# Two adaLN modulation vectors in the first stage of an encoder trunk: from a split between TensorE and VectorE to TensorE alone

## The chip, the cores and the metric

One NeuronCore of a Trainium2 chip runs the whole program in one launch. The metric is the device time of that launch in microseconds (us).

## The reference, cut to what matters

A trunk of two layers works on x of 256 tokens by 2048 channels, in float32. Layer 0 is RWKV-7 time mixing and a squared-ReLU MLP, layer 1 is chunked band attention and an MLP. Every sub-layer normalizes x and modulates it by vectors that come from one conditioning vector c of 2048 numbers:

```python
mod = c @ w_ada[layer] + b_ada[layer]            # 2048 x 12288 weights per layer
sh1, sc1, gt1, sh2, sc2, gt2 = jnp.split(mod, 6, axis=-1)
...
h = modulate(rms_norm(x, g_mix[layer]), sh1, sc1)   # h * (1 + sc1) + sh1
y = rwkv7_time_mix(h, ...)                          # r, k, v = xr @ w_r, xk @ w_k, xv @ w_v, each 2048 x 2048
x = x + gt1[:, None, :] * y
```

The change is to how `sh1` and `sc1` of layer 0 are computed: two products of the vector c with 2048 x 2048 weights, 32 MB of weights in all. Nothing of layer 0 can be projected before the first channels of both are there.

## The kernel before, in words

Channels lie on the 128 partitions, so 2048 channels are 16 tiles (`KT`), and a tile of x is 128 x 256. The program is written with tile pools; a planner gives every instruction its place on its engine and sets the waits, so that the order on an engine is not always that of the text.

The change lies in `layer_a`, in the first stage of the kernel. The stage loads x into `h`, sums squares over channels on TensorE (L726, operand `ones`), makes the reciprocal root `r` of the mean square (`rstd`, L526 to L533), and then loops over the 16 tiles n. For each n:

- two loads are issued on the SP queue, `lw` (L781, the low-rank weights) and `raw` (L368 from L782, the rows of `w_v` that belong to tile n);
- `h` is scaled by `gain` and `r` on VectorE (L788) and shifted on ScalarE (L790);
- GpSimd makes the token difference `xx` (L734), VectorE the mixes `mix` (L739) and their high and low halves (L572, with ScalarE's L571);
- the weights are split into a rounded half `wH` on ScalarE (L378) and a rest `wL` on VectorE (L381);
- TensorE multiplies: `l` in plain float32 (L797, L801), and `v` in three products per 128 x 128 block (L805 to L807, 24 per tile).

From n = 4 on, each turn also does one `v_part` (two in the last two turns, two more after the loop): 24 products `t` (L767 to L769) for the other half of v's columns, summed in two PSUM tiles tagged `t` and `m`, which have one bank each, and added into `v` by VectorE (L777) or copied by ScalarE (L775). Its weights are a `raw` load of `w_v`. The tag `m` is also what `self.psm()` hands out.

`gain` and the shift `mods[(0, 0)]` come from a generator, `ada_blocks`, which takes channels in blocks of two tiles (seven blocks) and of one (two blocks), called from ahead of the loop and in each turn. It splits the sum over c's 2048 entries:

- the first 1024 entries go to TensorE: a tile of `crep` (c repeated over 32 columns) is the held operand and the weights move, 256 or 128 columns of them, in four 128 x 32 column tiles (L690). The 128 partial rows are copied out by ScalarE (`adat`, L701) and summed over partitions by matmuls of one moving column (L706);
- the other 1024 entries go to VectorE: a transposed copy of those weights (`w_ada0_t`) is multiplied by `crow` and summed along the row (L696, into `sums`). `crow` is c laid out along the free axis, made once at the start by `diag` (L665), two matmuls (L670) and two copies (L671).

VectorE adds both and the bias (L711, L713) and makes the gain (L715). The weights arrive in buffers `rawa` of 128 x 1024, six of them, loaded on SP (L686, L695): 64 loads of 512 KB.

The other modulation vectors are computed later in the kernel by VectorE into `acc` (L454) and summed over partitions by matmuls of one moving column in 128 x 32 tiles (L476), 32 matmuls at a time. Stage 2 begins with the projections at L412 and L413.

Of the kernel before, what the change touches and what calls it, by code (L numbers as in the profile page):

```python
# [12 lines left out]
F32 = mybir.dt.float32  # L13
F32R = mybir.dt.float32r
AF = mybir.ActivationFunctionType
ALU = mybir.AluOpType
AX = mybir.AxisListType

P = 128
D = 2048  # L20
T = 256
KT = D // P
# [8 lines left out]
HK = 8  # L31
# [298 lines left out]
class Body:  # L330
# [303 lines left out]
    def layer_a(self, st, sp):  # L634
# [6 lines left out]
        with ExitStack() as s1:  # L641
# [9 lines left out]
            for q in range(4):  # L651
# [2 lines left out]
            nc.scalar.dma_start(out=self.bada, in_=d["b_ada"])  # L654
            nc.scalar.dma_start(out=self.vecs, in_=d["vecs"])
            nc.scalar.dma_start(out=self.csts[:, first:], in_=d["cst"][:, first:])
            crep = pb.tile([P, HK, 32], F32, name="crep")
            nc.vector.tensor_copy(crep, self.ct[:, :HK].unsqueeze(2).to_broadcast([P, HK, 32]))
            nc.vector.memset(h[:, :, 0:1], 0.0)
            gain = self.gp.tile([P, KT], F32, name="gain_g_mix0")  # L660
            sums = pb.tile([P, 2, KT], F32, name="sums01")
            rawa = lambda: pb.tile([P, HK * P], F32, tag="rawa", bufs=6, name="rawa")

            crow, diag = self.wp.tile([P, HK * P], F32, tag="acc", bufs=1, name="crow"), rawa()
            nc.vector.tensor_tensor(out=diag.rearrange("p (k n) -> p k n", n=P),  # L665
                                    in0=self.cst("ident").unsqueeze(1).to_broadcast([P, HK, P]),
                                    in1=self.ct[:, HK:].unsqueeze(2).to_broadcast([P, HK, P]), op=ALU.mult)
            for i in range(0, HK * P, 512):
                ps = pp.tile([P, 512], F32, tag="t", bufs=1, name="t")
                nc.tensor.matmul(ps, self.cst("ones"), diag[:, i:i + 512], start=True, stop=True)  # L670
                nc.scalar.copy(crow[:, i:i + 512], ps)  # L671

            blocks = [2] * 7 + [1] * 2

            def ada_blocks():


                lo = 0
                for w_ in blocks:
                    W, ks = w_ * P, HK // w_  # L680
                    ps = self.psm().rearrange("p (i n) -> p i n", i=2)
                    for part in (1, 0):
                        w = d["w_ada0"][:, part * D + lo * P:part * D + lo * P + W].rearrange("(a i p) n -> a p i n", p=P, i=ks)
                        for a in range(w_):
                            raw = rawa().rearrange("p (i n) -> p i n", i=ks)
                            nc.sync.dma_start(out=raw, in_=w[a])  # L686
                            for i in range(ks):
                                kt = ks * a + i
                                g = 32 * (kt % 4)
                                nc.tensor.matmul(ps[g:g + 32, part, :W], crep[:, kt, :], raw[:, i, :],  # L690
                                                 start=(part == 1 and kt < 4), stop=(part == 0 and kt >= HK - 4),
                                                 tile_position=(0, g))
                            yield
                            raw = rawa()
                            nc.sync.dma_start(out=raw, in_=d["w_ada0_t"][KT * part + lo + a])  # L695
                            nc.vector.scalar_tensor_tensor(out=raw, in0=raw, scalar=1.0, in1=crow, op0=ALU.mult,  # L696
                                                           op1=ALU.mult, accum_out=sums[:, part, lo + a:lo + a + 1])
                            if part or a < w_ - 1:
                                yield
                    t = pb.tile([P, 2 * T], F32, tag="adat", bufs=1, name="adat").rearrange("p (i n) -> p i n", i=2)  # L700
                    nc.scalar.copy(t[:, :, :W], ps[:, :, :W])  # L701
                    ps = self.psm()
                    for part in range(2):
                        for i in range(w_):
                            for g in range(0, P, 32):
                                nc.tensor.matmul(ps[g:g + 32, 2 * part + i:2 * part + i + 1],  # L706
                                                 t[:, part, i * P + g:i * P + g + 32], self.col(C_32ND),
                                                 start=True, stop=True, tile_position=(0, g))
                    o = slice(lo, lo + w_)
                    part_sums = sums[:, :, o]  # L710
                    nc.vector.tensor_tensor(out=part_sums, in0=part_sums,  # L711
                                            in1=self.bada[:, :2 * KT].rearrange("p (b k) -> p b k", b=2)[:, :, o], op=ALU.add)
                    nc.vector.tensor_tensor(out=self.mods01[:, :, o], in0=part_sums,  # L713
                                            in1=ps[:, :4].rearrange("p (b i) -> p b i", b=2)[:, :, :w_], op=ALU.add)
                    nc.vector.scalar_tensor_tensor(out=gain[:, o], in0=self.mods[(0, 1)][:, o], scalar=1.0,  # L715
                                                   in1=self.vec("g_mix0")[:, o], op0=ALU.add, op1=ALU.mult)
                    lo += w_
                    yield

            ends = [sum(blocks[:i + 1]) for i in range(len(blocks)) for _ in range(blocks[i])]  # L720
            adab = ada_blocks()
            ss = pp.tile([P, 2, T], F32, tag="v3", bufs=1, name="v3")[:, 0, :]
            for n in range(KT):
                sq = pb.tile([P, T], F32, tag="sq", bufs=3, name="sq")
                nc.scalar.activation(sq, h[:, n, 1:T + 1], AF.Square)
                nc.tensor.matmul(ss, self.cst("ones"), sq, start=(n == 0), stop=(n == KT - 1))  # L726
            r = self.rstd(ss)
            adab_at = 4 * ends[0]
            for i in range(adab_at):
                next(adab)  # L730

            def diff(n):
                xx = ph.tile([P, T], F32, tag="xx", bufs=2, name="xx")
# [45 lines left out]
            for n in range(KT):  # L779
                lw = pb.tile([P, 448], F32, tag="lw1", bufs=3, name="lw1")  # L780
                nc.sync.dma_start(out=lw, in_=d["lora1"][n // 4, :, n % 4, :])  # L781
                raw = self.raw(d["w_v_rows"][n])  # L782
                ahead = 5 if n + 2 < KT and ends[n + 1] == n + 2 else 0
                while adab_at < min(4 * KT, 4 * ends[min(n + 1, KT - 1)] + ahead):
                    next(adab)
                    adab_at += 1
                hn = h[:, n, 1:T + 1]
                nc.vector.scalar_tensor_tensor(out=hn, in0=hn, scalar=gain[:, n:n + 1], in1=r,  # L788
                                               op0=ALU.mult, op1=ALU.mult)
                nc.scalar.activation(hn, hn, AF.Identity, bias=self.mods[(0, 0)][:, n:n + 1])  # L790
                xx = diff(n)
                first, last = n == 0, n == KT - 1
                self.split(xv, n, mixed(3, n, xx))
                H, L = self.halves(raw)

                for i, m in enumerate((1, 4)):
                    nc.tensor.matmul(pl[0][:96, i, :], lw[:, i * 96:(i + 1) * 96], mixed(m, n, xx),  # L797
                                     start=first and i == 0, stop=last and i == 1)
                t = mixed(5, n, xx)
                for i in range(2):  # L800
                    nc.tensor.matmul(pl[1][:, i, :], lw[:, 192 + i * P:192 + (i + 1) * P], t,  # L801
                                     start=first and i == 0, stop=last and i == 1)
                for i in range(8):
                    ps = pv[i // 2][:, i % 2, :]
                    nc.tensor.matmul(ps, H[:, i, :], xv[:, n, 0, 0:T], start=first and i % 2 == 0, stop=False)  # L805
                    nc.tensor.matmul(ps, H[:, i, :], xv[:, n, 1, 0:T], start=False, stop=False)
                    nc.tensor.matmul(ps, L[:, i, :], xv[:, n, 0, 0:T], start=False, stop=last and i % 2 == 1)  # L807
                if n == 3:
                    self.v_next = v_part_weight()
                for _ in range((n >= 4) + (n >= KT - 2)):  # L810
                    v_part()
                self.split(xk, n, mixed(2, n, xx))

                nc.vector.scalar_tensor_tensor(out=hn, in0=xx, scalar=self.vec("mu0", n), in1=hn,
                                               op0=ALU.mult, op1=ALU.add)
# [347 lines left out]
def _arrange(x, c, w_ada, b_ada, g_mix, g_mlp, w_up, w_down,  # L1163
# [16 lines left out]
    for i, w in ((0, rwkv_w2), (1, rwkv_a2)):  # L1180
# [16 lines left out]
        "cst": CST,  # L1197
        "vecs": f(np.stack(vecs).reshape(len(VECS), KT, P).transpose(2, 0, 1)),
        "b_ada": f(np.concatenate([f(b_ada).reshape(-1), f(b_ada_kv).reshape(-1)]).reshape(-1, P).T),
        "w_ada0": f(w_ada[0][:HK * P, :2 * D]),  # L1200
        "w_ada0_t": f(w_ada[0][HK * P:, :2 * D].T).reshape(2 * KT, P, HK * P),
        "w_ada": f(w_ada), "w_ada_kv": f(w_ada_kv),
        "w_up": np.stack([_pack(w) for w in f(w_up)]),
        "w_down": np.stack([_pack(w) for w in f(w_down)]),
# [27 lines left out]
```

## Time and profile before

| | us |
|---|---|
| median of 3 runs | 2667.99 (2667.93 to 2668.28) |
| the profiled execution, time | 2668.82 |
| the profiled execution, span of the trace | 2667.0 |
| TensorE busy | 2594.2 |
| VectorE busy | 2112.8 |
| ScalarE busy | 1345.2 |
| GpSimd busy | 208.7 |

The span runs from the first to the last instruction of the trace. Engines are PE (TensorE matmuls), PEld (its weight loads), DVE (VectorE), ACT (ScalarE), POOL (GpSimd) and SP, whose queue issues most loads. A group of instructions is shown by line, engine, operation and operands, then its count, busy time, mean duration in ns, the idle time of the engine ahead of it and what ended that idle time. A matmul in plain float32 leaves two records. A matmul's record lasts longer than the distance to the next one, since they are pipelined, so costs on TensorE are read from the distances between starts.

### The profile page before, as it was taken

The numbers are of one execution on the slowest core, as the hardware profiler recorded it, in microseconds if no ns is written. First come the engines' busy times: TensorE is split into PE (matmuls) and PEld (weight loads), VectorE is DVE, ScalarE is ACT, GpSimd is POOL, SyncE is SP. The second block draws the span as 40 slices with busy tenths as digits, with TensorE's granted clock in tenths as the row PEclk, the third lists the DMA queues.
The fourth block names the chain that finished last, engine by engine and source line by source line (L and its number), as shares of the span: only waits on it lengthen the run. The fifth ranks groups of instructions, "written<-read, shape, count | busy, mean of one in ns | idle before, by whom it ended". The sixth has DMA issues, their size and how long they took to land.

```text
span 2667.0 us, 58173 instructions
## 1 busy us (share of the span) xinstructions
PE 2594.2 (97%) x23596; PEld 2229.2 (84%) x23596; DVE 2112.8 (79%) x3102; ACT 1345.2 (50%) x2435; POOL 208.7 (8%) x320
## 2 busy tenths in 40 slices
PE   7999999999999999999999999999999999999997
PEld 4787777887899888888888998877898888888886
DVE  6788888889789888888888898899887555555555
ACT  3346455555456445355365554565564463453554
POOL 0002223322110000000001100000100000000002
PEclk9999999999999999999999999999999999999998
DMA  9976556566778888889898679887766555555553
GB/s 349 312 244 211 185 179 207 180 214 199 246 236 312 309 317 327 319 324 332 318 329 293 238 242 331 318 274 256 265 218 235 190 189 184 188 189 186 186 189 119
DMA packets 207149, 662.62 MB, mean 248 GB/s; under 512 B 21408, under 2 KB 54560, under 8 KB 206880
## 3 DMA queue, kind: packets, MB, share of 16 engines
q1 hardware_dynamic: 204816, 656.36, 71.5%
q8 instruction: 185, 3.03, 0.5%
q10 hardware_dynamic: 2064, 2.54, 0.3%
q14 instruction: 84, 0.69, 0.1%
HBM read 656.72 MB, written 2.10 MB: 247 GB/s over the span
## 4 chain that ended last, share of the span: by engine, by line
PE 85%; DVE 5%; issue 4%; DMA 4%; ACT 2%; POOL 1%; DVEq 0%; SPq 0%; ACTq 0%; POOLq 0%
PE pj L412 45%; PE pj L413 23%; PE pj L402 2%; PE pj L401 2%; PE pj L403 2%; DMA raw<-w_ada 1%; DVE wL L381 1%; PE iv L111 1%; DVE acc L454 1%; PE gr L105 1%; ACT wH L378 1%; PE ms L115 1%; PE o L401 1%; PE ms L324 0%; PE ms L105 0%
## 5 line engine op out<-in xcount | busy, mean ns | idle before, releaser
L381 DVE TENSOR_TENSOR wL<-raw,wH 128x1024 fp32r<-128x1024 f32 x772 | 941.1, 1220 | 354.9 <-ACT wH L378 347.0
L378 ACT CAST wH<-raw 128x1024 fp32r<-128x1024 f32 x772 | 805.8, 1045 | 799.7 <-PE pj L412 650.0
L412 PE MATMUL pj<-aHL,wH 128*128 128x512 f32 x3328 | 1202.0, 403 | 1.9 <-DVE x L945 1.4
L413 PE MATMUL pj<-aHL,wL 128*128 128x256 f32 x3328 | 936.1, 281 | 0.4 <-DVE wL L381 0.4
L412 PEld LDWEIGHTS pj<-aHL,wH 128*128 128x128 f32 x3328 | 629.4, 189 | 154.4 <-issue 8.7
L412 PE MATMUL pj<-hHL,wH 128*128 128x512 f32 x2048 | 723.0, 398 | 0.0
L413 PEld LDWEIGHTS pj<-aHL,wL 128*128 128x128 f32 x3328 | 629.4, 189 | 3.1 <-issue 0.8
L413 PE MATMUL pj<-hHL,wL 128*128 128x256 f32 x2048 | 574.4, 281 | 0.0
L412 PEld LDWEIGHTS pj<-hHL,wH 128*128 128x128 f32 x2048 | 384.6, 188 | 94.4 <-DVE hHL L991 0.2
L413 PEld LDWEIGHTS pj<-hHL,wL 128*128 128x128 f32 x2048 | 386.8, 189 | 0.1
L454 DVE SCALAR_TENSOR_TENSOR acc<-rada,ct,acc 128x1024 f32<-128x1024 f32 x256 | 327.2, 1278 | 8.5 <-DMA rada<-w_ada 7.6
L518 POOL TENSOR_TENSOR ss<-ss,sq 128x256 f32<-128x256 f32 x56 | 52.6, 940 | 1590.8 <-ACT sq L517 1590.5
L1016 DVE SCALAR_TENSOR_TENSOR x<-pj,mod,x 128x256 f32<-128x256 f32 x256 | 123.4, 482 | 58.6 <-PE pj L413 54.9
L454 DVE SCALAR_TENSOR_TENSOR acc<-raw,ct,acc 128x1024 f32<-128x1024 f32 x104 | 136.2, 1309 | 15.3 <-DMA raw<-w_ada 14.9
L988 ACT ACTIVATE t<-t 128x256 f32<-128x256 f32 x112 | 46.8, 418 | 123.5 <-DVE t L960 123.5
L401 PE MATMUL pj<-aHL,wH 128*128 128x258 f32 x384 | 109.0, 284 | 0.0
L402 PE MATMUL pj<-aHL,wH 128*128 128x258 f32 x384 | 108.9, 284 | 0.0
L403 PE MATMUL pj<-aHL,wL 128*128 128x258 f32 x384 | 108.0, 281 | 0.0
L403 PEld LDWEIGHTS pj<-aHL,wL 128*128 128x128 f32 x384 | 73.2, 191 | 0.2
L402 PEld LDWEIGHTS pj<-aHL,wH 128*128 128x128 f32 x384 | 72.6, 189 | 0.1
L401 PEld LDWEIGHTS pj<-aHL,wH 128*128 128x128 f32 x384 | 72.2, 188 | 0.2
L990 ACT ACTIVATE t<-t 128x256 f32<-128x256 f32 x128 | 53.4, 417 | 3.4
(249 smaller groups left out, 2815.5 us busy)
## 6 DMA issues: line engine op xcount, KB each, us to landing
raw<-w_up SPq DMA_DIRECT2D x256, 512.0 KB, 4.2
raw<-w_down SPq DMA_DIRECT2D x256, 512.0 KB, 4.3
rada<-w_ada SPq DMA_DIRECT2D x209, 512.0 KB, 5.8
raw<-w_ada SPq DMA_DIRECT2D x111, 512.0 KB, 4.3
rada<-w_ada_kv SPq DMA_DIRECT2D x64, 512.0 KB, 6.1
rawa<-w_ada SPq DMA_DIRECT2D x32, 512.0 KB, 6.9
rawa<-w_ada_t SPq DMA_DIRECT2D x32, 512.0 KB, 7.5
raw<-w_k SPq DMA_DIRECT2D x32, 512.0 KB, 4.0
```

What stands on the lines that cost most here:

```text
L378: nc.scalar.copy(Hf, raw)
L381: eng.tensor_tensor(out=Lf, in0=raw, in1=Hf, op=ALU.subtract)
L401: nc.tensor.matmul(ps, H[:, i, :], a(kt)[:, 0, :], start=(first and kt == 0), stop=False)
L402: nc.tensor.matmul(ps, H[:, i, :], a(kt)[:, 1, :], start=False, stop=False)
L403: ins = nc.tensor.matmul(ps, L[:, i, :], a(kt)[:, 0, :], start=False, stop=(last and kt == KT - 1))
L412: nc.tensor.matmul(ps, H[:, i, :], a(kt), start=(kt == 0), stop=False)
L413: ins = nc.tensor.matmul(ps[:, 0, :], L[:, i, :], a(kt)[:, 0, :], start=False, stop=(kt == KT - 1))
L454: nc.vector.scalar_tensor_tensor(out=self.acc, in0=raw, scalar=ck, in1=self.acc, op0=ALU.mult, op1=ALU.add)
L518: (eng or nc.gpsimd).tensor_tensor(out=self.ss, in0=self.ss, in1=sq, op=ALU.add)
L988: nc.scalar.activation(t, t, AF.Relu)
L990: nc.scalar.activation(t, t, AF.Square)
L1016: nc.vector.scalar_tensor_tensor(out=x, in0=ps[:, i, :], scalar=self.mods[(layer, 5)][:, n:n + 1], in1=x, op0=ALU.mult, op1=ALU.add)
```

## The change

The generator, `crep`, `crow`, `diag`, `sums`, `adat` and the transposed copy of the weights go. A function `mods_tile(n)` computes both vectors for one channel tile on TensorE: the weights, packed so that a partition's row of a load is one run of 4 KB, are the held operand, cut into 128 x 32 tiles, and one column of c moves. All 16 blocks of c and both vectors' sums are accumulated in two columns of one PSUM tile. VectorE adds the bias and makes the gain. `rawa` has seven buffers. `mods_tile(0)` stands ahead of the loop, `mods_tile(n + 1)` in turn n.

```diff
-            crep = pb.tile([P, HK, 32], F32, name="crep")
-            nc.vector.tensor_copy(crep, self.ct[:, :HK].unsqueeze(2).to_broadcast([P, HK, 32]))
...
-            crow, diag = self.wp.tile([P, HK * P], F32, tag="acc", bufs=1, name="crow"), rawa()
-            nc.vector.tensor_tensor(out=diag.rearrange("p (k n) -> p k n", n=P), ...
-                nc.tensor.matmul(ps, self.cst("ones"), diag[:, i:i + 512], start=True, stop=True)
-                nc.scalar.copy(crow[:, i:i + 512], ps)
-            blocks = [2] * 7 + [1] * 2
-            def ada_blocks():
...
+            def mods_tile(n):
+                ps = self.psm()[:, :2]
+                for part in (1, 0):
+                    for a in range(KT // HK):
+                        raw = pb.tile([P, HK * P], F32, tag="rawa", bufs=7, name="rawa")
+                        nc.sync.dma_start(out=raw, in_=d["w_ada0"][KT * part + n][:, a * HK * P:(a + 1) * HK * P])
+                        for i in range(HK):
+                            kt = HK * a + i
                             for g in range(0, P, 32):
+                                nc.tensor.matmul(ps[g:g + 32, part:part + 1], raw[:, i * P + g:i * P + g + 32],
+                                                 self.ct[:, kt:kt + 1], start=(part == 1 and kt == 0),
+                                                 stop=(part == 0 and kt == KT - 1), tile_position=(0, g))
+                m = self.mods01[:, :, n]
+                nc.vector.tensor_tensor(out=m, in0=ps, in1=self.bada[:, :2 * KT].rearrange("p (b k) -> p b k", b=2)[:, :, n],
+                                        op=ALU.add)
+                o = slice(n, n + 1)
+                nc.vector.scalar_tensor_tensor(out=gain[:, o], in0=self.mods[(0, 1)][:, o], scalar=1.0,
+                                               in1=self.vec("g_mix0")[:, o], op0=ALU.add, op1=ALU.mult)
...
             r = self.rstd(ss)
-            adab_at = 4 * ends[0]
-            for i in range(adab_at):
-                next(adab)
+            mods_tile(0)
...
                 raw = self.raw(d["w_v_rows"][n])
-                ahead = 5 if n + 2 < KT and ends[n + 1] == n + 2 else 0
-                while adab_at < min(4 * KT, 4 * ends[min(n + 1, KT - 1)] + ahead):
-                    next(adab)
-                    adab_at += 1
+                if n < KT - 1:
+                    mods_tile(n + 1)
...
-        "w_ada0": f(w_ada[0][:HK * P, :2 * D]),
-        "w_ada0_t": f(w_ada[0][HK * P:, :2 * D].T).reshape(2 * KT, P, HK * P),
+        "w_ada0": _pack(w_ada[0][:, :2 * D]),
```

More of the change, by code (lines that the diff above doesn't have):

```diff
@@ L656, in layer_a @@
             nc.scalar.dma_start(out=self.csts[:, first:], in_=d["cst"][:, first:])
-            crep = pb.tile([P, HK, 32], F32, name="crep")
-            nc.vector.tensor_copy(crep, self.ct[:, :HK].unsqueeze(2).to_broadcast([P, HK, 32]))
             nc.vector.memset(h[:, :, 0:1], 0.0)
             gain = self.gp.tile([P, KT], F32, name="gain_g_mix0")
-            sums = pb.tile([P, 2, KT], F32, name="sums01")
-            rawa = lambda: pb.tile([P, HK * P], F32, tag="rawa", bufs=6, name="rawa")
@@ L664, in layer_a @@
-            crow, diag = self.wp.tile([P, HK * P], F32, tag="acc", bufs=1, name="crow"), rawa()
[L665 to L670, printed above, removed]
-                nc.scalar.copy(crow[:, i:i + 512], ps)
@@ L673, in layer_a @@
-            blocks = [2] * 7 + [1] * 2
-            def ada_blocks():
[L678 to L704, printed above, removed]
-                            for g in range(0, P, 32):
[L706 to L718, printed above, removed]
@@ L720, in layer_a @@
-            ends = [sum(blocks[:i + 1]) for i in range(len(blocks)) for _ in range(blocks[i])]
-            adab = ada_blocks()
+            def mods_tile(n):
[6 more added lines that the diff above has]
+                            kt = HK * a + i
+                            for g in range(0, P, 32):
+                                nc.tensor.matmul(ps[g:g + 32, part:part + 1], raw[:, i * P + g:i * P + g + 32],
[7 more added lines that the diff above has]
+                                               in1=self.vec("g_mix0")[:, o], op0=ALU.add, op1=ALU.mult)
```

## The prediction

> **What bounds the kernel now.** I read the page first, then the chain of waits that ended last, then the stretches of the stage that the change touches, then that stage's groups on TensorE (PE) and VectorE (DVE), and last the order in time around single bursts.
>
> ```profile
> PE 2594.2 (97%) x23596; PEld 2229.2 (84%) x23596; DVE 2112.8 (79%) x3102; ACT 1345.2 (50%) x2435; POOL 208.7 (8%) x320
> PE 85%; DVE 5%; issue 4%; DMA 4%; ACT 2%; POOL 1%; DVEq 0%; SPq 0%; ACTq 0%; POOLq 0%
> 0.00:32.61 32.61, 18.21 (x117) 10.01 (x117) 13.21 (x26) 12.46 (x26) 2.38 (x6) 0.94 0.91 314
> 32.61:66.37 33.76, 28.87 (x253) 22.34 (x249) 28.60 (x61) 11.05 (x19) 3.78 (x4) 0.90 1.05 382
> 66.37:173.03 106.66, 97.22 (x904) 78.28 (x904) 87.64 (x173) 35.46 (x58) 7.22 (x9) 0.98 0.90 309
> 66.37:203.10 136.73, 124.67 (x1112) 104.17 (x1112) 110.39 (x207) 53.36 (x82) 8.14 (x10) 0.99 0.81 276
> ```
>
> The first row is busy time by engine, the second the chain by engine: the kernel is a TensorE kernel. The others are stretches: length, busy us of PE, PEld, DVE, ACT and POOL, the granted clock of PE, the share of the DMA engines and GB/s. The cuts are where the first `l` matmul of tile 0 starts (32.61), that of tile 4 (66.37), that of tile 14 (173.03), and stage 2's first matmul (203.10). After 203.10 the program is the same, so what the stage gains or loses is taken as what the kernel does. From 66.37 to 173.03 three things run close together: PE 97.2 of 106.7 us, DVE 87.6, DMA 0.90. DMA is not the limit there, having moved 382 GB/s in the stretch before against 309.
>
> A busy PE hides waiting, so its need is counted from starts. Groups from 66.37 to 203.10 (busy, mean ns, idle before and who ended it):
>
> ```profile
> L767 PE MATMUL t<-aHL,wH 128*128 128x256 f32 x125 | 36.6, 293 | 5.6 <-DVE v L777 4.2 <-ACT v L775 1.3
> L769 PE MATMUL t<-aHL,wL 128*128 128x256 f32 x125 | 36.1, 290 | 4.2 <-DVE wL L381 4.2
> L806 PE MATMUL v<-aHL,wH 128*128 128x256 f32 x96 | 27.3, 294 | 0.0
> L797 PE MATMUL l<-mix,lw 128*96 128x256 f32 x48 | 13.6, 405 | 2.6 <-DVE mix L739 2.6
> L690 PE MATMUL m<-rawa,crep 128*32 128x256 f32 x128 | 10.7, 406 | 0.0
> L690 PE MATMUL m<-rawa,crep 128*32 128x128 f32 x64 | 2.6, 279 | 0.0
> L706 PE MATMUL m<-csts,adat 128*32 128x1 f32 x160 | 2.3, 173 | 0.3 <-ACT adat L701 0.3
> ```
>
> And the order in time on PE (start, length, count), around a burst of L690, around one of L706, and over one tile's `l`:
>
> ```profile
> 71.91 0.28 PE L806 MATMUL v<-aHL,wH 128*128 128x256 f32 x1
> 72.02 0.28 PE L807 MATMUL v<-aHL,wL 128*128 128x256 f32 x1
> 72.23 0.64 PE L690 MATMUL m<-rawa,crep 128*32 128x256 f32 x8
> 73.02 0.29 PE L807 MATMUL v<-aHL,wL 128*128 128x256 f32 x1
> ...
> 105.78 0.28 PE L805 MATMUL v<-aHL,wH 128*128 128x256 f32 x1
> 105.99 0.43 PE L706 MATMUL m<-csts,adat 128*32 128x1 f32 x32
> 106.58 0.28 PE L807 MATMUL v<-aHL,wL 128*128 128x256 f32 x1
> ...
> 98.42 1.02 PE L797 MATMUL l<-mix,lw 128*96 128x256 f32 x4
> 100.20 0.39 PE L767 MATMUL t<-aHL,wH 128*128 128x256 f32 x1
> ```
>
> Main matmuls start 0.12 apart. Between the last one ahead of the L690 burst (72.02) and the second after it (73.02) lie 1.00 us where two steps, 0.24, would do: a burst of eight costs 0.76, entering and leaving included. By the same reading a burst of L706 costs 0.80 - 0.24 = 0.56. A tile's `l` takes 100.20 - 98.42 = 1.78, say 1.9 with the slower step behind it.
>
> Need of PE from 66.37 to 203.10: 375 `t` (L768 is as many as its neighbours) and 288 `v` at 0.12, 79.6; 12 tiles' `l`, 22.8; 16 bursts of eight and 4 of sixteen at L690, 15.2 at 0.76; six bursts of L706, 3.4 at 0.56. Sum 121.0 of 136.7. So 15.7 is waiting, and 11.0 of it stands in the rows as waits for DVE (4.2, 4.2 and 2.6).
>
> **The change part by part.** *Removed from DVE:* the products at L696.
>
> ```profile
> L696 DVE SCALAR_TENSOR_TENSOR rawa<-rawa,crow 128x1024 f32<-128x1024 f32 x20 | 24.0, 1217 | 0.0
> ```
>
> That is 24.0 of DVE's 87.6 us up to tile 14, leaving 64 of 107, 60%. The small adds (two a tile in place of three a block) stay near nothing. ScalarE loses the copies `adat` and `crow`; it is under half busy, so that pays nothing by itself.
>
> *Removed from PE:* L690 and L706, 15.2 + 3.4 = 18.6 us for tiles 6 to 15 in this stretch.
>
> *Added to PE:* per tile 2 x 16 x 4 = 128 matmuls with one moving column, 256 records, in four loads of 64 records. The nearest work is L476, which has the same form and sends 64 records at once:
>
> ```profile
> 1176.52 0.28 PE L413 MATMUL pj<-aHL,wL 128*128 128x256 f32 x1
> 1176.87 0.28 PE L413 MATMUL pj<-aHL,wL 128*128 128x256 f32 x1
> 1177.08 0.71 PE L476 MATMUL m<-csts,acc 128*32 128x1 f32 x64
> 1178.06 0.28 PE L413 MATMUL pj<-aHL,wL 128*128 128x256 f32 x1
> ...
> 1177.58 0.20 PE L476 MATMUL m<-csts,acc 128*32 128x1 f32 x3
> 1177.62 0.17 PE L476 MATMUL m<-csts,acc 128*32 128x1 f32 x1
> ```
>
> From L413 to L413 across the burst is 1.19, without it 0.35: 0.84 a burst. Inside, (0.71 - 0.17) / 63 = 0.0086 a record. The last two rows are the same burst cut short at its front: its last three records lie (0.20 - 0.17) / 2 = 0.015 to (1177.62 - 1177.58) / 2 = 0.02 apart, twice the mean. I read that as a stock of instructions, waiting when the burst began, that has run out by then. So a tile costs 4 x 0.84 = 3.36 if its four bursts stand alone, 0.84 + 192 x 0.017 = 4.1 if they join and the slow step holds, and 0.84 + 192 x 0.0086 = 2.5 if they join and the fast one does. I take 3.36, since every L690 burst above stands alone between other matmuls, each behind its own load; 2.5 and 4.1 stay for the range. All sums of a tile go into two columns; L476's records, two to a sum, show no price for that.
>
> [...]
>
> *From 66.37 on, after:* 79.6 + 22.8 + 10 tiles x 3.36 = 136.0 with no wait at all, already the present 136.7. For waits I take 8 of the present 15.7: DVE's 11.0 halved as its load falls, the rest left; ends 3 and 13. Result 144.0, +7.3.
>
> *From 32.61 to 66.37:* the rows there, cold clock included (0.90 granted):
>
> ```profile
> L805 PE MATMUL v<-aHL,wH 128*128 128x256 f32 x32 | 9.9, 336 | 0.0
> L797 PE MATMUL l<-mix,lw 128*96 128x256 f32 x16 | 5.7, 491 | 2.7 <-DVE mix L739 2.7
> L690 PE MATMUL m<-rawa,crep 128*32 128x256 f32 x52 | 4.9, 447 | 0.0
> L769 PE MATMUL t<-aHL,wL 128*128 128x256 f32 x3 | 0.9, 316 | 1.6 <-DVE wL L381 1.6
> L706 PE MATMUL m<-csts,adat 128*32 128x1 f32 x64 | 0.9, 173 | 0.0
> ```
>
> Four tiles: 96 `v` and 9 `t` at 0.12, 12.6; `l` 7.6; 6.5 bursts of L690, 4.9; two of L706, 1.1: 26.2 of 33.8, 7.6 lost. After: 20.2 + 4 x 3.36 = 33.6, with 5 lost (ends 3 and 7.6) 38.6, +4.8.
>
> *Ahead of 32.61:*
>
> ```profile
> 13.35 1.91 PE L670 MATMUL t<-rawa,csts 128*128 128x512 f32 x2
> ```
>
> ```profile
> 26.36 1.22 DVE L696 SCALAR_TENSOR_TENSOR rawa<-rawa,crow 128x1024 f32<-128x1024 f32 x1
> 27.50 0.42 DVE L533 SCALAR_TENSOR_TENSOR rstd<-ru,rstd 128x256 f32<-128x256 f32 x1
> ```
>
> `crow`'s matmuls stand among the sums of squares (1.9), and the last step of `r` stands behind an L696 (1.1). Both go, and the first gain needs 2 MB of weights, not 4. I take 4 us earlier (0 to 6); what is late next is the loads, 7.9 MB by the second tile (x 2.1, constants and the first turn's loads 1.6, eight of `rawa` 4.2), 25 us at the 314 GB/s of that stretch.
>
> *Moved:* 64 loads of 512 KB stay 64 on SP, four in a row and ahead of the same turn's `w_v` load. They now wait for PE alone to free a buffer, seven in place of six; `lw` and both `raw` loads are queued behind that wait, and ScalarE's and VectorE's splits wait for these. `mods_tile` also takes the one bank `m` from `v_part` and must wait for L777; behind it on PE are `l`, `v` and the next `v_part`. Both are inside the waits above.
>
> *Sum.* With c the price of a tile: late 10c - 26.3, early 4c - 8.6, start -4, together 14c - 38.9. For c = 3.36 that is +8.1. The span goes from 2667.0 to 2675.1; the profiled execution took 2668.8 against a median of 2668.0, so the forecast goes on the median: 2676.1. Its own range, by waits 3 to 13 and 3 to 7.6 and a start 0 to 6 earlier: 2669 to 2688.
>
> **The rivals.** *Faster:* VectorE is the real pace-setter, the bursts join at 0.0086 (c = 2.5), and waits fall to 3 late and 4 early: 14c - 44.9 = -9.9, 2658. It decides below c = 3.2. For it: the 11.0 us of waits for DVE. Against: the slow last records, and L690's bursts that never join.
>
> *No change:* c = 3.36 with the same low waits, and a start 6 earlier: 14c - 46.9 = +0.1, 2668. For it: PE needs only 121 of 137 now. Against: `m`, the loads and the split of `raw` still make PE wait.
>
> *Fed too slowly:* bursts join, and the slow step rules: c = 4.1 gives +18.5, and at 0.02 a record c = 4.7 gives +27; 2691 in the middle. For it: the last three records. Against: it needs loads that are there ahead of time. [...]
>
> **How the numbers follow.** About 0.2%, 5 us, is what a measurement of this kernel can tell from no change. Chances: forecast 0.58 (0.50 slower, 0.08 within), faster 0.13 (0.12 faster, 0.01 within), no change 0.17 (0.14 within, 0.02 slower, 0.01 faster), fed too slowly 0.12. Together 0.13 faster, 0.23 the same, 0.64 slower. The range 2660 to 2697 leaves out some 0.07 below and 0.06 above.
>
> **What would show it.** Right: L696, L690 and L701 gone; 4096 records of one column on PE; a burst of 64 with 0.84 between its neighbours; DVE near 60% in the loop; waits for DVE under 6 us; stage 2's first matmul near 211 and the first `l` near 28.6. Wrong: joined bursts at under 0.01 a record, or that first matmul before 203 (faster); records 0.015 apart or more (slower still); or a difference that arises after stage 2 begins, which I take as none.

## The result, and the profile after

The changed kernel takes 2730.25 us (median of four, 2722.72 to 2733.2) against 2667.96 of the kernel before: ratio 1.023, interval 1.0208 to 1.0253. It is 62 us slower; 8 were forecast, and the time lies outside the range of 2660 to 2697. The profiled execution took 2733.2 us, with a span of 2731.4.

From the page of the changed kernel, busy time by engine and the row of TensorE's instruction queue (packets, MB):

```profile
PE 2636.2 (97%) x27144; PEld 2282.8 (84%) x27144; DVE 2073.2 (76%) x3041; ACT 1340.4 (49%) x2424; POOL 212.5 (8%) x320
...
q8 instruction: 213, 3.49, 0.5%
```

The same queue on the page of before:

```profile
q8 instruction: 185, 3.03, 0.5%
```

TensorE has 3548 matmul records and as many weight loads more, some 7100 instructions; its queue fetched 28 packets more, 0.46 MB, so a packet is 16 KB and holds about 256 instructions, and 185 of them fit the 47192 records of before.

Nearly all of the loss lies in the stage that was changed (62.0 of the 64.4 us between the two profiled spans). Stage 2's first matmul starts at 265.04 (before 203.09). The first `l` starts at 36.1 (before 32.6, +3.5), tile 4's at 82.5: the early stretch, from the first `l` to tile 4's, takes 46.4 (33.8, +12.6), the late one, from there to stage 2, 182.5 (136.7, +45.8). The stretches of the changed kernel, cut about there, and below them three around one place of it (length, busy us of PE, PEld, DVE, ACT and POOL, granted clock, DMA share, GB/s):

```profile
0.00:34.50 34.50, 15.97 (x543) 13.59 (x544) 3.68 (x9) 9.69 (x21) 0.83 (x5) 0.90 0.91 323
34.50:83.00 48.50, 38.76 (x919) 33.93 (x915) 22.11 (x52) 10.38 (x18) 3.87 (x4) 0.79 0.69 241
83.00:265.00 182.00, 157.71 (x3574) 142.03 (x3573) 89.61 (x170) 51.51 (x76) 10.13 (x11) 0.86 0.62 211
...
101.00:106.00 5.00, 1.49 (x63) 1.39 (x53) 0.50 (x3) 0.00 (x0) 0.00 (x0) 0.66 0.90 347
106.00:116.00 10.00, 9.32 (x172) 8.18 (x171) 5.93 (x11) 3.70 (x6) 0.92 (x1) 0.83 0.34 101
116.00:129.00 13.00, 12.98 (x426) 11.20 (x427) 6.34 (x13) 3.70 (x6) 0.92 (x1) 1.00 0.86 306
```

VectorE is busy 49% of the late stretch, the DMA share has fallen to 0.62, and the granted clock from 0.99 to 0.86. So neither of the old neighbours of the bound holds the stage now. The waits from 20 to 265 us (us in total, times, longest):

```profile
DVE mods L673 <- PE m L669: 89.1, 16, 8.6
...
PEld m L669 <- issue: 35.9, 28, 4.6
PE m L669 <- issue: 29.3, 10, 4.6
...
PE t L722 <- DVE v L732: 1.5, 1, 1.5
PE t L722 <- ACT v L730: 1.4, 2, 0.7
```

TensorE hardly waits for VectorE any more. It stands mostly in front of its own new matmuls and waits for nothing that the trace shows ("issue"). The order in time on PE shows one such place (start, length, count), and, later, bursts that run through:

```profile
100.45 0.28 PE L758 MATMUL v<-aHL,wH 128*128 128x256 f32 x1
100.57 0.28 PE L759 MATMUL v<-aHL,wH 128*128 128x256 f32 x1
100.78 0.47 PE L669 MATMUL m<-ct,rawa 128*32 128x1 f32 x34
104.77 0.60 PE L669 MATMUL m<-ct,rawa 128*32 128x1 f32 x30 [3.51 <-issue]
105.30 0.58 PE L760 MATMUL v<-aHL,wL 128*128 128x256 f32 x1
105.68 0.41 PE L758 MATMUL v<-aHL,wH 128*128 128x256 f32 x1
...
188.41 0.28 PE L758 MATMUL v<-aHL,wH 128*128 128x256 f32 x1
188.62 0.71 PE L669 MATMUL m<-ct,rawa 128*32 128x1 f32 x64
189.26 0.67 PE L750 MATMUL l<-mix,lw 128*96 128x256 f32 x2
```

The burst at 188.62 (a burst is a run of such matmuls) takes 0.85 from the `v` ahead of it to the `l` behind. The one at 100.78 stops after 34 of its 64 records, though they read one load that is there, and goes on 3.7 us later. Counting PE's instructions from the start of the trace (matmuls, weight loads and its few semaphore instructions), this stop comes after 4033 of them, which is 193 more than a multiple of 256. There are 13 stops of 1.8 to 4.7 us, from the last start ahead to the first behind, and all come 193 past a multiple of 256; they take 38.6 us in all. Ten are inside bursts, three between main matmuls shortly behind one. The kernel before has no stop of 1 us or more at that place in this stage. In the stop at 101 the instruction queue fetched one packet (row of its queue from 101 to 106):

```profile
q8 instruction: 1, 0.02, 1.2%
```

It landed 1.4 us ahead of the next record. In each of the 13 stops one packet of that queue landed, 1.2 to 1.6 us ahead of the next record. Behind the stop the main matmuls start 0.21 apart, not 0.12, until 109.3: the granted clock of the rows 101 to 116, 0.66 and 0.83, and 0.50 from 102.7 to 109.4. I call a run of 256 instructions a block, and a stop at place 193 one at a block's end.

### The profile page after: what moved, and what is told of

It is laid out like the page before. It is cut to its first block, busy times and chain, and to the rows that moved or that the text cites. A ratio compares the mean times of both kernels' runs of the same rounds, so it can differ in the third digit from the quotient of the medians.

```text
span 2731.4 us, 65181 instructions
## 1 busy us (share of the span) xinstructions
PE 2636.2 (97%) x27144; PEld 2282.8 (84%) x27144; DVE 2073.2 (76%) x3041; ACT 1340.4 (49%) x2424; POOL 212.5 (8%) x320
## 4 chain that ended last, share of the span: by engine, by line
PE 87%; DVE 5%; DMA 3%; issue 3%; ACT 1%; POOL 0%; DVEq 0%; SPq 0%; ACTq 0%
PE pj L412 44%; PE pj L413 22%; DMA raw<-w_ada 2%; PE pj L402 2%; PE pj L401 2%; PE pj L403 2%; PE m L669 2%; DVE acc L454 2%; PE iv L111 1%; DVE wL L381 1%; PE v L758 1%; PE v L759 1%; PE gr L105 1%; PE v L760 1%; PE t L722 1%
## 5 line engine op out<-in xcount | busy, mean ns | idle before, releaser
L412 PEld LDWEIGHTS pj<-aHL,wH 128*128 128x128 f32 x3328 | 629.5, 189 | 153.1 <-issue 8.2
L941 ACT ACTIVATE t<-t 128x256 f32<-128x256 f32 x112 | 46.8, 418 | 123.7 <-DVE t L913 123.7
L669 PEld LDWEIGHTS m<-ct,rawa 128*32 128x32 f32 x4096 | 44.0, 117 | 54.0 <-issue 45.2
L669 PE MATMUL m<-ct,rawa 128*32 128x1 f32 x4096 | 50.0, 175 | 39.7 <-issue 29.3
L402 PEld LDWEIGHTS pj<-aHL,wH 128*128 128x128 f32 x384 | 72.6, 189 | 0.1
```

Source lines behind the costliest of these rows:

```text
L402: nc.tensor.matmul(ps, H[:, i, :], a(kt)[:, 1, :], start=False, stop=False)
L412: nc.tensor.matmul(ps, H[:, i, :], a(kt), start=(kt == 0), stop=False)
L669: nc.tensor.matmul(ps[g:g + 32, part:part + 1], raw[:, i * P + g:i * P + g + 32], self.ct[:, kt:kt + 1], start=(part == 1 and kt == 0), st ...
L941: nc.scalar.activation(t, t, AF.Relu)
```

## The experiments

Edits are shown against the changed kernel, where no other is named.

**Half the price.** Every second block of c is left out.

```diff
-                        for i in range(HK):
+                        for i in range(0, HK, 2):
...
-                                                 stop=(part == 0 and kt == KT - 1), tile_position=(0, g))
+                                                 stop=(part == 0 and kt == KT - 2), tile_position=(0, g))
```

> The changed kernel with every second of c's 16 blocks left out of the two vectors; all 64 loads stay. Three theories of the 62 us. Supply: PE's instructions arrive in blocks of 256, about one per 5.8 us in this stage, and a turn of the loop needs 512 for the vectors and some 150 for the rest; halved, a turn needs 1.6 blocks, 9.3 us, less than PE's own 9.9, so the gaps at every 256th instruction nearly go: 2660 to 2675. Burst price (the prediction's c): bursts of 32 records at 0.56 in place of 0.84, 14 tiles x 1.12 = 16 us less than the changed kernel: 2714. Late loads: nothing changes, 2730.

Measured 2683.79 us, ratio 1.006 [1.0037, 1.0083]. One stop at a block's end is left (2.3 us at 22.9). The first `l` starts at 27.7, 4.9 earlier than before. So three quarters of the loss go with half the instructions, far more than a price by the record would give back; nearest is the theory of supply, but 16 us stay with hardly a stop, and no theory had that. Late waits of this run (63 to 224):

```profile
DVE mods L673 <- PE m L669: 49.5, 11, 5.6
...
PE t L722 <- DVE v L732: 8.6, 8, 1.4
PE l L750 <- DVE mix L694: 8.6, 10, 1.5
```

The order in time of one turn shows how they hang together:

```profile
123.19 0.43 PE L669 MATMUL m<-ct,rawa 128*32 128x1 f32 x32
...
123.70 0.16 DVE L673 TENSOR_TENSOR mods<-m,bada 128x2 f32<-128x2 f32 x1 [5.45 <-PE m L669]
...
124.09 0.48 DVE L741 SCALAR_TENSOR_TENSOR h<-h,gain_g_mix,rstd 128x256 f32<-128x256 f32 x1
...
127.27 1.27 DVE L694 SCALAR_TENSOR_TENSOR mix<-xx,vecs,h 128x256 f32<-128x256 f32 x3
```

VectorE stands 5.45 us for a tile's last burst, with `h`, the mixes and the adds into `v` queued behind; that tile's `l` follows 5 us after the burst. The last two experiments take this up.

**Held operands of 128 columns,** a quarter of the matmuls.

```diff
-                            for g in range(0, P, 32):
-                                nc.tensor.matmul(ps[g:g + 32, part:part + 1], raw[:, i * P + g:i * P + g + 32],
...
+                            nc.tensor.matmul(ps[:, part:part + 1], raw[:, i * P:(i + 1) * P],
...
```

> The changed kernel with one 128x128 held operand per block in place of four 128x32: same sums, a quarter of the matmuls (64 records a tile, not 256). Supply: no gap at every 256th instruction; what is left is the price of a tile, unknown for a 128-column load before one moving column, 0.06 to 0.12 a record, c of 4 to 8, and with 14c - 38.9 that is 2685 to 2741; PE's clock returns to 1.0. Burst price: the changed kernel plus 14 x (c - 3.36), 2739 to 2795. Late loads: 2730.

One run, 2846.93 us, slower than anything expected: all theories missed. No stop at a block's end is left, but a record is dear. Two stretches, and two bursts in order of time:

```profile
32.00:70.00 38.00, 36.24 (x182) 34.53 (x183) 13.13 (x31) 5.32 (x10) 1.87 (x3) 0.59 0.43 150
70.00:180.00 110.00, 98.56 (x567) 91.85 (x566) 31.17 (x66) 16.49 (x27) 3.06 (x5) 0.70 0.45 154
```

```profile
121.01 1.84 PE L668 MATMUL m<-ct,rawa 128*128 128x1 f32 x16
...
139.37 2.77 PE L668 MATMUL m<-ct,rawa 128*128 128x1 f32 x13
```

Inside the first the records start 0.112 us apart, inside the second 0.213 (the main matmuls ahead of it start 0.21 apart, those ahead of the first 0.12), against 0.0084 in 128 x 32 tiles; and PE, busy nearly all the time, is granted only 0.59 to 0.70. So this run says nothing on the supply of instructions. Why the clock falls there was not tried.

**No loads.** Tile 0's weights serve all tiles; the loads of the other fifteen are left out.

```diff
-                        raw = pb.tile([P, HK * P], F32, tag="rawa", bufs=7, name="rawa")
-                        nc.sync.dma_start(out=raw, in_=d["w_ada0"][KT * part + n][:, a * HK * P:(a + 1) * HK * P])
+                        if n == 0:
+                            kept[part, a] = pb.tile([P, HK * P], F32, name=f"rawa{part}{a}")
+                            nc.sync.dma_start(out=kept[part, a], ...)
+                        raw = kept[part, a]
```

> The changed kernel with the weights of tile 0 used for all 16 tiles, loaded once: 60 of 64 loads are left out, the instructions on PE stay. Supply, with the blocks' arrival slowed by the loads beside them: gaps stay at every 256th instruction but shrink, 2680 to 2705; supply that does not depend on the loads: 2725 to 2735. Burst price: 2725 to 2735 with no gaps inside bursts. Late loads: 2680 or less, no gaps.

One run, 2718.7 us: 30 MB less to load bring some 12 us. It lies between the two forms of the theory of supply (2680 to 2705, 2725 to 2735). Fifteen stops are left, all at the same place of a block, 1.2 to 3.6 us, 39.2 in all. Three of them follow on one another (PE in order of time):

```profile
28.83 1.89 PE L673 MATMUL m<-ct,rawa 128*32 128x1 f32 x128 [3.39 <-issue]
32.28 1.07 PE L673 MATMUL m<-ct,rawa 128*32 128x1 f32 x66 [1.57 <-issue]
...
35.74 1.45 PE L673 MATMUL m<-ct,rawa 128*32 128x1 f32 x94 [1.10 <-issue]
```

With the data at hand, 128 matmul records and 128 weight loads, a block, start every 3.45 us. So the stops need no late loads of these weights. That loads lengthen them is possible: the packets that end the stops start on average 1.5 us after the block before has begun to run here (counted from its place 193), and 3.4 us after that in the changed kernel.

**The disputed cost by itself.** The kernel before, with bursts of 16, 32, 64, 128 and 256 matmuls of the same form on constants, put between the projections of the MLPs, far from the changed stage.

```diff
+                if q == 2 and n in (2, 5, 8, 11, 14):
+                    pm, ones = self.psm(), self.cst("ones")
+                    for k in range(4 << (n // 3)):
+                        for i in range(0, P, 32):
+                            nc.tensor.matmul(pm[i:i + 32, 0:1], ones[:, i:i + 32], self.col(C_ONE), ...
```

> The kernel before with extra bursts of the change's form (128x32 held constants, one moving column, no load behind them) in the third quarter of both MLPs' down projections: 16, 32, 64, 128 and 256 matmuls, that is 32 to 512 records, with 128x128 work between them. Burst price at 0.017 a record beyond 64: 0.56, 0.84, 1.9, 4.1 and 8.5 us, 32 us in both layers, 2700; at 0.0086: 20 us, 2688. Supply of PE's instructions in blocks of 256, one per some 3.5 us when PE waits for them (the steps between the gaps where tile 0's weights were reused): no gap up to 64 records, then one for each block that runs out: the burst of 512 records, four blocks, takes 11 to 15 us, that of 256 some 4 to 8; 2700 to 2715, about alike in layer 0, where loads run at 320 GB/s, and layer 1, at 187.

One run, 2725.39 us. PE in order of time, around the bursts of 128 and 256 records in the first MLP and of 512 in the second:

```profile
1286.44 1.25 PE L1018 MATMUL m<-csts 128*32 128x1 f32 x128
1287.62 0.50 PE L412 MATMUL pj<-hHL,wH 128*128 128x512 f32 x1
...
1305.60 1.81 PE L1018 MATMUL m<-csts 128*32 128x1 f32 x197
1312.51 1.02 PE L1018 MATMUL m<-csts 128*32 128x1 f32 x59 [5.09 <-issue]
1313.46 0.79 PE L412 MATMUL pj<-hHL,wH 128*128 128x512 f32 x1
...
2507.80 1.48 PE L1018 MATMUL m<-csts 128*32 128x1 f32 x157
2512.62 1.88 PE L1018 MATMUL m<-csts 128*32 128x1 f32 x128 [3.34 <-issue]
2516.10 1.89 PE L1018 MATMUL m<-csts 128*32 128x1 f32 x128 [1.59 <-issue]
2519.58 1.55 PE L1018 MATMUL m<-csts 128*32 128x1 f32 x99 [1.59 <-issue]
```

128 records run through, from first to last start 1.07 us, 0.0084 each: only the last two steps are longer, 0.017, as they are in a burst of 64. The 256 stop after 197 (after 253 in the second MLP, 2.8 us), the 512 after 157. From then on exactly 128 records run and then 1.6 us pass: a block every 3.48 us (2512.62 to 2516.10 to 2519.58), the 1.9 of its own records included (1.25 in the burst at 1286.44). Each of these packets starts 1.1 us after the block before has begun to run and takes 1.0 us, and 1.4 us after it has landed the next record starts. So the price is a step: in these bursts nothing for the first 157 to 253 records, one to two blocks with their weight loads, and then a stop of 3 to 5 us and 1.6 to 1.9 at each block after that. This carries the theory of supply.

The time is 57 us above the kernel before, 10 above the highest that was expected. The eight stops take 24 of it and the 1984 records 17 at 0.0084. What is left, 16, was not taken apart; the clock rows of the trace show half clock for 48 us around these stops.

**TensorE alone, with few instructions:** the old form (L690's), `crep` held and the weights moving, for all sixteen blocks of c, six buffers.

```diff
-            def mods_tile(n):
...
+            blocks = [2] * 7 + [1] * 2
+            def ada_blocks():
...
+                        for a in range(2 * w_):
...
+                                nc.tensor.matmul(ps[g:g + 32, part, :W], crep[:, kt, :], raw[:, i, :],
+                                                 start=(part == 1 and kt < 4), stop=(part == 0 and kt >= KT - 4),
```

> VectorE left out as in the change, but by the form the kernel before has for its first half: all 16 blocks of c held, repeated over 32 columns, and the weights moving, 256 columns a matmul (six buffers). PE's price of a tile is the same as forecast for the change: eight bursts at 0.76 and one at 0.56 for two tiles, c = 3.3, but a quarter of the instructions. Supply: no gap at every 256th instruction; 14c - 38.9 is +8, and the longer waits for VectorE's mixes and sums that halving left (10 us more than before) may be in it: 2672 to 2690. If price or VectorE's absence alone made the 62 us: 2720 or more.

Measured 2686.87 us, ratio 1.0075 [1.0047, 1.0103]. No stop at a block's end; stage 2 begins at 221.8. The stretch from 66 on, and its idle times on PE:

```profile
66.00:222.00 156.00, 146.77 (x1400) 115.92 (x1399) 91.90 (x168) 57.21 (x88) 10.98 (x12) 0.98 0.80 259
```

```profile
L749 PE MATMUL t<-aHL,wH 128*128 128x256 f32 x128 | 38.1, 298 | 6.3 <-DVE v L759 4.1 <-ACT v L757 1.6 <-ACT wH L378 0.5
L751 PE MATMUL t<-aHL,wL 128*128 128x256 f32 x128 | 36.6, 289 | 1.5 <-DVE wL L381 1.5
...
L779 PE MATMUL l<-mix,lw 128*96 128x256 f32 x50 | 14.6, 408 | 1.2 <-DVE mix L721 1.2
```

So taking VectorE's share to TensorE costs 18.7 us in itself, late at 0.98 of the clock and with the 9.0 us of waits in these rows; the held form, with its order by single tiles in place of blocks of two, costs 43.6 more (62.3 - 18.7).

**A hybrid:** the held form for the first eight blocks of c, VectorE's products for the other eight.

```diff
-                    for a in range(KT // HK):
+                    for a in range(1):
...
+                    nc.vector.scalar_tensor_tensor(out=raw, in0=raw, scalar=1.0, in1=crow, op0=ALU.mult,
+                                                   op1=ALU.mult, accum_out=sums[:, part, n:n + 1])
```

> The change for the first 8 blocks of c only, the other 8 on VectorE as in the kernel before (same loads, seven buffers): 128 records a tile on PE in two bursts, c = 1.7 against 1.8 before, VectorE as full as before. Supply: 256 instructions a tile as in the halved run, gaps nearly gone: 2662 to 2685. Burst price: 2666. Late loads: as before, 2668. VectorE the pace-setter in the kernel before: 2668, and the halved run's 16 us come from the order of work, not from PE.

Measured 2668.27 us, ratio 1.0002 [0.9987, 1.0017]: with 256 instructions a tile the loss is gone, even with two stops left (3.77 at 25.1, 4.51 at 47.9). Every theory had allowed about this time, so the run decides between none of them.

**Longer matmuls:** 32 equal columns of c move in place of one.

```diff
-                                nc.tensor.matmul(ps[g:g + 32, part:part + 1], raw[:, i * P + g:i * P + g + 32],
-                                                 self.ct[:, kt:kt + 1], ...
+                                nc.tensor.matmul(wide[g:g + 32, part, :], raw[:, i * P + g:i * P + g + 32],
+                                                 crep[:, kt, :], ...
```

> The changed kernel with 32 equal moving columns in place of one: the same 2048 matmuls and instructions, each longer. Supply: the longer matmuls run in time that PE would have waited, 2720 to 2740. Burst price: the four-record step of 0.034 grows by 32 columns in two passes, c rises by 1 to 3, 2745 to 2775.

One run, 2722.82 us, within the spread of the changed kernel (2722.72 to 2733.2). Thirty-two times the columns for the same instructions cost nothing that one run can show. Its 20 stops, at the same place of a block, take more than in the changed kernel (55.7 us against 38.6), while half clock behind the first `l` is less (34 us against 65). What is not lost to the clock is lost in stops. That fits a stage that goes by the blocks' arrival: the number of instructions is what is paid.

**Bursts spread:** the same matmuls, one vector at the start of a turn, the other, two tiles ahead, at its end.

```diff
-                    mods_tile(n + 1)
+                    mods_part(n + 1, 0)
...
+                if n < KT - 2:
+                    mods_part(n + 2, 1)
```

> The changed kernel with the same 2048 matmuls in another order: one vector of the next tile at the start of a turn, the other, of the tile after, at its end, each with its own sum and add, so that no more than 256 of PE's instructions for the vectors stand close together. Supply as a matter of bursts (about one block ahead, then 2.9 us for each more): gaps fewer and shorter, 2690 to 2712. Supply as a matter of the total (2.5 blocks a turn at 5.8 us): 2722 or more. Burst price: 2730.

Measured 2723.86 us, ratio 1.0202 [1.0184, 1.0221]. Sixteen stops at the same place of a block, smaller (29.6 us in all), but nearly all of the loss stays, as the expectation by the total has it. The order still keeps 256 instructions close together, a block's worth; a finer spread was not tried.

**Hybrid, first four tiles as in the kernel before.**

```diff
+            blocks = [2] * 2
+            def ada_blocks():
...
+                    raw = rawa()
+                    nc.sync.dma_start(out=raw, in_=d["w_ada0_p"][KT * part + n][:, :HK * P])
+                    for kt in range(HK):
...
```

> The half-and-half kernel of the run before (held weights for c's first 8 blocks, VectorE for the rest) with its first four tiles made as in the kernel before (moving weights, blocks of two), six buffers. Supply: the half-and-half run still had two gaps at a 256th instruction, 3.8 us at 25 and 4.5 us at 48, each followed by a half clock; with few instructions early both go, 2655 to 2664. If those gaps were slack that something else would have filled: 2665 to 2670, no change.

Measured 2665.87 us, ratio 0.998 [0.997, 0.9991]. The two stops of the hybrid are gone and five short ones (1.0 to 1.4) have come. It is the only version below the kernel before, by 0.2%, 5 us against the kernel before measured beside it (2670.82). By its time it falls under "no change" (2665 to 2670), by the ratio at the low end of the 4 to 13 us that the stops seemed to be worth.

**Two turns ahead,** for the half-price kernel, the changed kernel and the hybrid alike.

```diff
-                if n < KT - 1:
-                    mods_tile(n + 1)
+                if n == 0:
+                    mods_tile(1)
+                if n < KT - 2:
+                    mods_tile(n + 2)
```

> Every second block of c left out, as before (256 instructions a tile on TensorE in place of 512), and each tile's vectors computed two turns ahead of their use in place of one. With one turn the half-price kernel took 2683.8 against 2667.9 of the kernel before, although its blocks of instructions arrive in time; in its stretch 63.4 to 223.6 VectorE stood up to 5.6 us at a time for the sums of the next tile, and behind it gain, h, xx, the mixes and then l. Theory of the chain: what is left of the loss is this chain from a tile's last burst to its l, which one turn can't hide; two turns ahead it is hidden, and the time falls to 2658 to 2672, with the waits of l for mix (8.6 us) under 3. Rival, the price: bursts and granted clock hold the stage at about 220 whatever their order, 2680 to 2688.

> The changed kernel as it is, only each tile's vectors two turns ahead of their use. Theory of supply (blocks of 256 instructions on TensorE come too slowly for three bursts and what lies between them): the same instructions at the same mean rate, gaps at 192 or 193 of 256 as before and 25 to 45 us in sum, 2710 to 2732. Theory of the chain (most of the 62 us are tiles whose vectors come too late for their turn, the gaps being hidden otherwise): 2680 to 2700.

> TensorE has the first eight blocks of c with held weights, VectorE the other eight, each tile two turns ahead in place of one. With one turn: 2668.3, the same as the kernel before. By the chain two turns take away its waits of l for mix (5.7 us) and part of t's for v (7.3): 2655 to 2664. If the loads or the two gaps at a block's end set it (8.3 us in sum, both early), no change: 2665 to 2671.

The half-price kernel: 2678.77 us, ratio 1.0035 [1.0021, 1.0049], against 1.006 with one turn. Late waits (63 to 222):

```profile
PE t L724 <- DVE wL L381: 8.6, 11, 1.4
...
PE t L722 <- DVE v L732: 1.4, 2, 0.8
```

The wait of `l` for `mix` no longer shows there, and `t`'s for `v` fell from 8.6 to 1.4; but the split of the weights, queued behind on VectorE, is now late (2.9 before, 8.6 now). So the chain from the burst to `l` is some 7 of the 16 us by the ratios (5 by the medians); the expected 2658 to 2672 did not come, and the other 9 are open. The changed kernel: 2728.57 us, as without, with twelve stops and 33.3 us in them: as supply has it, the chain none of it. The hybrid: 2677.27 us, ratio 1.003 [1.0018, 1.0041], 9 slower than with one turn, outside both expectations; its `t` now waits 9.5 us for `wL`, its first `l` starts at 35.5 behind a stop of 4.6.

## Why the prediction was wrong

The direction was right, and several steps held. The 4096 records came as forecast, and L696, L690 and L701 are gone. A burst of 64 that runs through costs 0.83 (0.84 forecast): 0.85 from the `v` ahead to the `v` behind and 0.22 to the next, less two steps of 0.12. They stand alone after the start. VectorE fell to 49% (60% forecast), and the waits for VectorE are under 6.

**The step that failed is the price of a tile, c.** It was read from bursts of 64 records, and taken as a cost of each record. The runs show a cost by blocks: c = 3.36 holds for bursts without a stop (0.83 each), and a late turn of the loop now has 512 instructions for the vectors and some 112 for the rest (24 `v`, 24 `t` and 8 records of `l`, each with its weight load): 2.4 blocks. Before it had 444 less (7100 / 16): 0.7. At 3.48 a block that would be 8.5 us, less than the 11 that such a turn needs (48 x 0.12 + 1.9 + 3.36). But in front of the 13 stops a block was through in 1.3 to 4.4 us, and the next began 3.5 to 7.3 us after it had begun (median 6.0). At 6.0 the 2.4 blocks take 14.6, near the 15.2 of a late turn (182.5 / 12). Why a block takes longer here than 3.48, and how much of the loss is the mean rate and how much the uneven use, is open. The term of the sum that was mis-sized is that of the late stretch, +7.3, which measured +45.8. By the forecast's need of 136.0, 46.5 of the 182.5 us are lost: 22.8 in eight stops, and by the one at 101 about 2 more each, 16 together, at half clock behind them (an estimate: 18 matmuls at 0.21 in place of 0.12, and half a burst). The clock rows give an upper bound: half clock for 42 us outside these stops, which would cost 21. That leaves 3 to 8 for all other waits, where 8 were taken. The early stretch has 9.0 us of stops in its 46.4 (38.6 forecast).

**The start was to gain 4 us and lost 3.5.** Two stops, 4.40 and 2.31, lie ahead of the first `l`; 36.1 less these is 29.4, near the 28.6 forecast. In the half-price kernel, with one stop of 2.3 there, it started at 27.7.

**The rival "fed too slowly"** had the right cause, instructions that run out, with the wrong form. It read a slow step of 0.015 to 0.02 from the last three records of a burst of L476, as a stock that has run out. The burst of 128 shows the same step at its own end and 0.0084 ahead of it, so the step belongs to the end of a burst, and that reading was wrong. Nor did it need joined bursts: three of the 13 stops come between main matmuls. Hence its 2691 was too low as well.

The forecast's own range was added up wrongly at its lower end: 2676.1 less 5, 2 and 2 is 2667, not 2669. That changes nothing here.

**What the page of before did show:** 185 packets on TensorE's instruction queue, for 23596 matmul records and as many weight loads. The prediction counted the time of 256 records a tile, and never the instructions as something to be fetched. Nor did it have a row for more than 64 records at a stretch; the range should have been open on that side.

**The waits taken for a TensorE that is fed** were too low. By the forecast's formula half the price (c = 2.2 for four bursts of 0.55) gives 14 x 2.2 - 38.9 = -8; the half-price kernel lost 16. About 5 to 7 of these 24 were the chain from a tile's last burst over VectorE, ScalarE and GpSimd to its `l`, which the old blocks of two tiles had kept a turn further ahead. Of the rest the runs show where TensorE waits (for `wL`, in VectorE's order), but not why.

## What to carry to other kernels

Count a tiny float32 matmul not by its length but by its four instructions, two records with a weight load each (2048 matmuls left 4096 of both here). A lone run of 256 instructions between long matmuls was free of stops (the burst of 128 records at 1286.44); behind a stop each further 256 took some 3.5 us in that run, and the blocks at the 13 stops of the changed kernel 3.5 to 7.3. I would put many-instruction work on TensorE only with long matmuls between the bursts (with half the instructions a turn one of the 13 stops was left), and price it by instructions in a turn, with the queue's packets on the page as the measure. A price read from a short burst was too low for a longer one here: at 0.84 for 64 records, 256 would take 3.4 us, and they took 7.9 (1305.60 to 1313.46).

## What was not expected of the hardware

A held operand of 128 columns with one moving column takes 0.112 us a record where main matmuls start 0.12 apart, 13 times the 0.0084 of a 128 x 32 tile, and the stage full of them was granted 0.59 of the clock from 32 to 70 us, with PE busy for 36.2 of 38, and 0.70 from 70 to 180, with 98.6 of 110. At the stops the granted clock fell as well: at each of the 13 the trace shows half clock (0.50), which held in the stop or began at most 1.3 us behind it, and the matmuls behind the stop at 101 ran at 0.21 apart for 4 us. And moving 32 columns in place of one, 4096 times, could not be seen in the time of one run (2722.82).
